# Rotary scores of multi-head latent attention: two mixed passes as one matmul, with high parts of the queries moved across partitions by transfers

## The chip, the core and the metric

The kernel runs on one core of one Trainium2 chip. Its engines are TensorE (PE, with its weight loads shown apart as PEld), VectorE (DVE), ScalarE (ACT), GpSimd (POOL) and SyncE (SP), each with a queue of its own that is worked off in order. The metric is the time of one execution on the device, in us.

## The reference, cut to what matters

One layer of an encoder over 256 tokens of width 2048, in float32: multi-head latent attention (MLA, 8 heads) and differential attention side by side, cross attention into 256 memory tokens, a gated feed-forward block and a last norm. The part that the change touches are MLA's scores. Each head has a part of 128 dimensions without rotation and a rotary part of 64, and all heads share one rotary key:

```python
q_rope = apply_rope(q[..., MLA_NOPE_DIM:], cos_r, sin_r)
k_rope = apply_rope(k_rope, cos_r, sin_r)
...
s = (jnp.einsum('bqhd,bkhd->bhqk', qn_b, k_nope)
     + jnp.einsum('bqhr,bkr->bhqk', qr_b, k_rope))
p = jax.nn.softmax(s.astype(jnp.float32) * scale, axis=-1).astype(v.dtype)
return jnp.einsum('bhqk,bkhd->bqhd', p, v)
```

## The kernel before

**Three passes.** Every float32 product is made on PE in the format float32r from two parts of each operand: h is the value rounded by ACT (L99, L102), l is what is left, subtracted by DVE (L100, L103). `mm` issues h x h, h x l and l x h into one PSUM sum (L91, L92, L93). `Split` is such a pair of tiles, `split_into` makes it, `act_tile` takes two buffers for it from the pool "act", which has 24 buffers of one size (128 partitions x 1024 float32).

**The steps of MLA.** The first projection gives the latents; `latents_normalized` norms them, rotates the shared key (`kr`) and transposes all to dimension-major form: cqT (queries' latent), and in one tile `lat` ckvT (keys' and values' latent) and krT (rotary key). `kr` is 256 wide with the key in columns 0 to 63 and again in 192 to 255 and zeros between, so krT has two planes: plane 0 has the key in partitions 0 to 63 and zeros in 64 to 127, plane 1 the other way round. The rotary queries of all heads come from one projection, are rotated (`qrs`) and transposed into qrT: plane j of qrT holds head 2j in partitions 0 to 63 and head 2j + 1 in 64 to 127. A head's rotary score takes the plane of its pair and the plane of krT for its parity; the zeros cut out the other head. So a head's scores are, for each of the two token tiles, three passes for the 128 dimensions (qT, kT) and three for the rotary part (qrT, krT).

The heads come in two groups of four (`hg`). For each group `stationary` makes qT and kT and `values` makes the values (tiles `val_h`, `val_l`, read out of the PSUM tiles `acc`). Then, pair of heads by pair, `scores` fills a PSUM tile psc, `softmax` takes the maximum (nm, DVE), the exponential (e, ACT, with its sum ssum), the reciprocal (rs) and scales (DVE); `prob_T` transposes the result on PE (ppt, L462 before, L495 after) and splits it into pT; `heads_out` multiplies with the values (po) into mixT.

**What stands around it.** acc_dq, the first projection of differential attention, is held in two of the four PSUM banks of the pool "pacc" until `diff_rope` reads it, after MLA's last value split (`issue_after(mla_split)`). The other two banks serve, one after the other, the rotary queries, the two groups' values and then the projection of dk (`diff_project(0, 1)`, matmuls acc<-..x0T), which is independent of MLA.

**What sets the order.** The kernel is written in Tile, and its scheduler puts the instructions of each engine in an order of its own by a time model, at build time; weight loads alone stay as written (`keep_in_program_order`). Buffers of a pool are given in the order in which tiles are asked for, and a tile whose buffer is still read by an earlier one waits for that reader. So the number of tiles asked for can change the order of all engines.

Of the kernel before, what the change touches and what calls it, by code (L numbers as in the profile page):

```python
# [11 lines left out]
F32 = mybir.dt.float32  # L12
F32R = mybir.dt.float32r
# [3 lines left out]
ALU = mybir.AluOpType  # L17
AX = mybir.AxisListType

P = 128  # L20
S = 256
# [9 lines left out]
DD = 128  # L31
DV = 256
XH = 4
# [41 lines left out]
def encoder_block(ctx: ExitStack, tc: tile.TileContext, a, out):  # L75
# [13 lines left out]
    def mm(o, l, r, start, stop):  # L89

        nc.tensor.matmul(o, l.h, r.h, start=start, stop=False)  # L91
        nc.tensor.matmul(o, l.h, r.l, start=False, stop=False)  # L92
        nc.tensor.matmul(o, l.l, r.h, start=False, stop=stop)  # L93
# [13 lines left out]
    def act_tile(shape=(P, 4, S), name="act"):  # L107
        return Split(
            act.tile(list(shape), F32R, name=name + "_h", tag="act"),
            act.tile(list(shape), F32R, name=name + "_l", tag="act"),  # L110
        )
# [57 lines left out]
    def ps_tile(name):  # L169
        return pps.tile([P, 512], F32, name=name, tag="ps")  # L170
# [140 lines left out]
    def transposed(dst, src, tt, n, gain=None, raw=None):  # L311

        pt = ps_tile("pt")
        for j in range(n):
            nc.tensor.transpose(out=pt[:, j * P:(j + 1) * P], in_=src[:, j * P:(j + 1) * P], identity=ident)  # L315
        pv = pt[:, :n * P].rearrange("p (j t) -> p j t", t=P)
        if gain is not None:
            g = nat("gT").rearrange("p (j t) -> p j t", t=P) if raw is None else raw[:, :, tt * P:(tt + 1) * P]
            nc.vector.tensor_tensor(out=g[:, :n, :], in0=pv, in1=gain.unsqueeze(2).to_broadcast([P, n, P]),
                                    op=ALU.mult)  # L320
            pv = g[:, :n, :]
        split_into(dst[:, :n, tt * P:(tt + 1) * P], pv)
# [27 lines left out]
    cosd = const.tile([P, NT, 2, DD // 2], F32, name="cosd")  # L350
    sind = const.tile([P, NT, 2, DD // 2], F32, name="sind")

    def latents_normalized():
        cqs = [nat("cq") for _ in range(NT)]
        for tt in range(NT):
            rms_rows(cqs[tt], acc_q[tt], tt, QL, QL, "rq")
        with tc.issue_after(last_cast[0]):
            for c_t, s_t, f0, f1 in ((cosr, sinr, 0, DR // 2), (cosd, sind, DR // 2, NF)):
                for h in range(2):
                    nc.scalar.activation(s_t[:, :, h, :], turns[:, :, f0:f1], AF.Sin, scale=two_pi if h else -two_pi)  # L360
                    nc.scalar.activation(c_t[:, :, h, :], prod[:, :, f0:f1], AF.Sin, scale=two_pi)
        for t in (cosd, sind):
            for tt in range(NT):
                nc.gpsimd.tensor_scalar(out=t[:, tt], in0=t[:, tt], scalar1=rstd1[:, tt:tt + 1], scalar2=None,
                                        op0=ALU.mult)
        ckvs = [nat("ckv") for _ in range(NT)]
        for tt in range(NT):
            rms_rows(ckvs[tt], acc_kv[tt], tt, KVL + DR, KVL, "rkv")
        for tt in range(NT):
            transposed(cqT, cqs[tt], tt, 4, g_q)  # L370
        for tt in range(NT):
            c = ckvs[tt]

            kr = nat("kr")
            nc.gpsimd.memset(kr[:, 64:192], 0.0)
            rope(kr[:, 0:64], c[:, 256:320], cosr[:, tt], sinr[:, tt], 1, 32)
            nc.gpsimd.tensor_copy(out=kr[:, 192:256], in_=kr[:, 0:64])
            transposed(ckvT, c, tt, 2, g_kv)
            transposed(krT, kr, tt, 2)


    acc_dq = project(x0T, [w_in[0, i] for i in range(4)], before=lambda i: i == 3 and latents_normalized())
# [32 lines left out]
            split_into(t[:, 2 * hp:2 * hp + 2, :], ps.rearrange("p (j t) -> p j t", j=2))  # L415
        return t

    qrT = act_tile(name="qrT")
    acc = project(lambda kt: cqT[:, kt, :], [a["w_uq_r"]])
    qrs = []  # L420
    for tt in range(NT):
        qr = nat("qr")
        rope(qr, acc[tt], cosr[:, tt], sinr[:, tt], NH, 32)
        qrs.append(qr)
    qT, kT, vv = [], [], []
    for hg in range(2):
        qT.append(stationary(weights(a["w_uq_n"][hg]), cqT, 4, "qT"))
        if hg == 0:
            for tt in range(NT):
                transposed(qrT, qrs[tt], tt, 4)  # L430
        kT.append(stationary(weights(a["w_ukv_k"][hg]), ckvT, 2, "kT"))
        vv.append(values(project(lambda kt: ckvT[:, kt, :], [a["w_ukv_v"][hg]])))
    mla_split = last_split[0]

    def scores(qs, ks):

        ps = ps_tile("psc")
        for tt in range(NT):
            for n, (q, k) in enumerate(zip(qs, ks)):
                mm(ps[:, tt * S:(tt + 1) * S], q[:, tt * P:(tt + 1) * P], k, n == 0, n == len(qs) - 1)  # L440
        return ps.rearrange("p (t k) -> p t k", t=NT)

    def softmax_parts(ps, scale):

        nm = small.tile([P, NT], F32, name="nm", tag="nm", bufs=4)
        nc.vector.tensor_reduce(out=nm, in_=ps, axis=AX.X, op=ALU.max, negate=True)
        nc.vector.tensor_scalar(out=nm, in0=nm, scalar1=scale, scalar2=None, op0=ALU.mult)
        e = soft.tile([P, NT, S], F32, name="e", tag="e", bufs=4)
        ssum = small.tile([P, NT], F32, name="ssum", tag="ssum", bufs=4)
        for tt in range(NT):  # L450
            nc.scalar.activation(e[:, tt, :], ps[:, tt, :], AF.Exp, bias=nm[:, tt:tt + 1], scale=scale,
                                 accum_out=ssum[:, tt:tt + 1])
        r = small.tile([P, NT], F32, name="rs", tag="rs", bufs=4)
        nc.vector.reciprocal(out=r, in_=ssum)
        return e, r
# [31 lines left out]
    for hg in range(2):  # L487
        t = act_tile(name="mixT")
        mixT.append(t)
        for hp in range(2):  # L490
            ps = [scores([qT[hg][:, h, :], qrT[:, 2 * hg + hp, :]], [kT[hg][:, h, :], krT[:, h % 2, :]])
                  for h in (2 * hp, 2 * hp + 1)]
            pTs = [prob_T(softmax(s, (DN + DR) ** -0.5)) for s in ps]
            heads_out(t[:, 2 * hp:2 * hp + 2, :], pTs, vv[hg], 2 * hp)
# [17 lines left out]
    def diff_attend(dq, dk, dv):  # L512
        mT = act_tile(name="diffT")
        ps_ = []
        for hh in range(2):
            (e1, r1), (e2, r2) = [
                softmax_parts(scores([dq[:, 2 * hh + c, :]], [dk[:, 2 * hh + c, :]]), DD ** -0.5) for c in range(2)]
            nr2 = small.tile([P, NT], F32, name="nr2", tag="nr2")
            nc.vector.tensor_scalar(out=nr2, in0=r2, scalar1=neg_lam, scalar2=None, op0=ALU.mult)
            for tt in range(NT):  # L520
                nc.vector.tensor_scalar(out=e1[:, tt, :], in0=e1[:, tt, :], scalar1=r1[:, tt:tt + 1], scalar2=None,
                                        op0=ALU.mult)
                nc.vector.scalar_tensor_tensor(out=e1[:, tt, :], in0=e2[:, tt, :], scalar=nr2[:, tt:tt + 1],
                                               in1=e1[:, tt, :], op0=ALU.mult, op1=ALU.add)
            ps_.append(e1)
        for hh in range(2):
            pT = prob_T(ps_[hh])
            po = ps_tile("pod")
            for tt in range(NT):
                for kt in range(NT):  # L530
                    mm(po[:, tt * DV:(tt + 1) * DV], pT[:, kt, tt * P:(tt + 1) * P],
                       dv[:, kt, hh * DV:(hh + 1) * DV], kt == 0, kt == NT - 1)
            ss = small.tile([P, NT], F32, name="ssd", tag="ssd")
            for tt in range(NT):
                meansq(po[:, tt * DV:(tt + 1) * DV], ss[:, tt:tt + 1], DV, DV)
            r = rstd_of(ss, 1e-5, "rd")
            on = nat("on")
            for tt in range(NT):
                nc.vector.scalar_tensor_tensor(out=on[:, tt * DV:(tt + 1) * DV], in0=po[:, tt * DV:(tt + 1) * DV],
                                               scalar=r[:, tt:tt + 1], in1=gdb, op0=ALU.mult, op1=ALU.mult)  # L540
            pt = ps_tile("pdt")
            for e in range(2):
                for tt in range(NT):
                    nc.tensor.transpose(out=pt[:, e * S + tt * P:e * S + (tt + 1) * P],
                                        in_=on[:, tt * DV + e * P:tt * DV + (e + 1) * P], identity=ident)
            split_into(mT[:, 2 * hh:2 * hh + 2, :], pt.rearrange("p (e t) -> p e t", e=2))
        return mT
# [71 lines left out]
        transposed(xqT, n, tt, 4)  # L619

    pxT = [act_tile(name="pxT") for _ in range(2)]
    ps = [scores([xqT[:, h, :]], [xkT[:, h, :]]) for h in range(XH)]
    for h in range(XH):
        prob_T(softmax(ps[h], XD ** -0.5), pxT[h // 2][:, h % 2 * 2:h % 2 * 2 + 2, :])
    xv = values(project(mT, [a["w_xv"][i] for i in range(4)]), rstdm)
# [380 lines left out]
```

## Time and profile before

| | |
|---|---|
| median of 3 runs | 1158.89 us (1158.38 to 1160.23) |
| the profiled execution: time of the run | 1158.9 us |
| the profiled execution: span | 1157.1 us |
| PE busy | 1148.1 us, 99%, 5510 matmuls |
| DVE busy | 901.3 us, 78% |
| ACT busy | 611.0 us, 53% |
| POOL busy | 69.3 us, 6% |
| granted TensorE clock over the span | 0.999 |

The span is counted from the first to the last instruction of the program; the run's time has 1.8 us around it. Busy times of PE overlap: matmuls are pipelined, and what one costs in a full queue is the distance between starts. In rows of the timeline the columns are start and duration in us, engine, line, operation, output tile and input tiles, shapes, count, and in brackets the idle time before it and what ended it. In the list of waits the columns are total us, times, and the longest.

### The profile page before, as it was taken

How to read it: one execution, taken by the hardware profiler on the slowest of the kernel's cores; microseconds unless marked ns; L12 is line 12 of the kernel's file. 1: busy time of each engine (PE TensorE's matmuls, PEld its weight loads, DVE VectorE, ACT ScalarE, POOL GpSimd, SP SyncE). 2: the span in 40 equal slices, each digit the busy share in tenths (PEclk: the TensorE clock that was granted, in tenths of full speed). 3: DMA queues.
4: the chain of work that ended last, by engine and by line, in shares of the span. 5: the costliest groups of instructions: out<-in, count | busy, mean ns of one | idle time of the engine just before them, and what ended most of it. 6: DMA issues, size and time to landing. Idle time of an engine off the chain costs nothing.

```text
span 1157.1 us, 14401 instructions
## 1 busy us (share of the span) xinstructions
PE 1148.1 (99%) x5510; PEld 961.7 (83%) x5510; DVE 901.3 (78%) x1197; ACT 611.0 (53%) x863; POOL 69.3 (6%) x81
## 2 busy tenths in 40 slices
PE   9999999999999999999999999999999999999997
PEld 7888888888888888888888888888888888888887
DVE  7698766586867776978888787797888788798873
ACT  6755454554665565655444554564544554554552
POOL 4920000001000000000000000000000000000021
PEclk9999999999999999999999999999999999999999
DMA  9565344435755445465565555645556555555651
GB/s 356 215 218 189 113 145 168 161 146 206 272 212 182 146 149 187 174 218 182 185 214 184 206 184 192 218 181 183 202 179 223 204 181 202 192 220 202 210 204 73
DMA packets 33764, 222.13 MB, mean 192 GB/s; under 512 B 4128, under 2 KB 4896, under 8 KB 8992
## 3 DMA queue, kind: packets, MB, share of 16 engines
q1 hardware_dynamic: 32256, 216.86, 52.4%
q0 software_dynamic: 864, 3.15, 0.7%
q10 hardware_dynamic: 576, 1.21, 0.3%
q8 instruction: 43, 0.70, 0.2%
q14 instruction: 25, 0.20, 0.1%
HBM read 219.11 MB, written 2.10 MB: 191 GB/s over the span
## 4 chain that ended last, share of the span: by engine, by line
PE 98%; DMA 1%; issue 0%; DVE 0%; SPq 0%; ACT 0%; POOLq 0%; POOL 0%; DVEq 0%; ACTq 0%
PE acc L92 28%; PE acc L91 28%; PE acc L93 28%; PE q L91 2%; PE q L92 2%; PE q L93 2%; PE pt L315 2%; PE ppt L462 1%; DMA wraw<-in_w_in_lat 1%; PE psc L93 1%; PE psc L91 1%; PE psc L92 1%; PE pt L838 0%; PE acckv L93 0%; PE acckv L92 0%
## 5 line engine op out<-in xcount | busy, mean ns | idle before, releaser
L99 ACT CAST wh<-wraw 128x1024 fp32r<-128x1024 f32 (+2 forms) x399 | 399.2, 1013 | 383.1 <-PE acc L93 346.7
L100 DVE TENSOR_TENSOR wl<-wraw,wh 128x1024 fp32r<-128x1024 f32 (+2 forms) x399 | 469.0, 1184 | 166.3 <-ACT wh L99 164.4
L92 PE MATMUL acc<-wl,x2n_h 128*128 128x512 f32 x480 | 185.5, 390 | 0.0
L93 PE MATMUL acc<-wh,x2n_l 128*128 128x512 f32 x480 | 185.2, 389 | 0.0
L91 PE MATMUL acc<-wh,x2n_h 128*128 128x512 f32 x480 | 160.3, 390 | 0.0
L93 PEld LDWEIGHTS acc<-wh,x2n_l 128*128 128x128 f32 x480 | 90.1, 188 | 18.8
L91 PEld LDWEIGHTS acc<-wh,x2n_h 128*128 128x128 f32 x480 | 90.1, 188 | 18.8
L92 PEld LDWEIGHTS acc<-wl,x2n_h 128*128 128x128 f32 x480 | 90.1, 188 | 18.7
L92 PE MATMUL acc<-wl,hT_h 128*128 128x512 f32 (+1 forms) x272 | 103.7, 381 | 0.0
L93 PE MATMUL acc<-wh,hT_l 128*128 128x512 f32 (+1 forms) x272 | 103.5, 381 | 0.0
L91 PE MATMUL acc<-wh,hT_h 128*128 128x512 f32 (+1 forms) x272 | 89.4, 382 | 0.0
L92 PE MATMUL acc<-wl,x0T_h 128*128 128x512 f32 x224 | 88.2, 395 | 0.0
L93 PE MATMUL acc<-wh,x0T_l 128*128 128x512 f32 x224 | 87.8, 393 | 0.0
L91 PE MATMUL acc<-wh,x0T_h 128*128 128x512 f32 x224 | 87.4, 396 | 0.3 <-ACT x0T_h L102 0.3
L99 ACT CAST wh<-tsum 128x1024 fp32r<-128x1024 f32 x56 | 58.3, 1047 | 42.2 <-DVE tsum L712 30.8
L100 DVE TENSOR_TENSOR wl<-tsum,wh 128x1024 fp32r<-128x1024 f32 x56 | 67.9, 1218 | 9.2 <-ACT wh L99 9.1
L91 PEld LDWEIGHTS acc<-wh,hT_h 128*128 128x128 f32 x272 | 51.2, 188 | 9.9 <-issue 0.2
L93 PEld LDWEIGHTS acc<-wh,hT_l 128*128 128x128 f32 x272 | 51.2, 188 | 9.6
L92 PEld LDWEIGHTS acc<-wl,hT_h 128*128 128x128 f32 x272 | 51.2, 188 | 9.4
L91 PEld LDWEIGHTS acc<-wh,x0T_h 128*128 128x128 f32 x224 | 42.2, 189 | 9.2 <-ACT x0T_h L102 1.2
L92 PEld LDWEIGHTS acc<-wl,x0T_h 128*128 128x128 f32 x224 | 42.3, 189 | 7.9 <-DVE wl L100 0.4
L93 PEld LDWEIGHTS acc<-wh,x0T_l 128*128 128x128 f32 x224 | 42.2, 188 | 7.6
(363 smaller groups left out, 2005.9 us busy)
## 6 DMA issues: line engine op xcount, KB each, us to landing
wraw<-in_w_gu SPq DMA_DIRECT2D x80, 1024.0 KB, 4.8
wraw<-in_w_dn SPq DMA_DIRECT2D x36, 1024.0 KB, 4.8
wraw<-in_w_in SPq DMA_DIRECT2D x24, 1024.0 KB, 4.8
wraw<-in_w_out SPq DMA_DIRECT2D x16, 1024.0 KB, 4.8
wraw<-in_w_down SPq DMA_DIRECT2D x8, 1024.0 KB, 4.8
wraw<-in_w_in_lat SPq DMA_DIRECT2D x7, 832.0 KB, 7.8
wraw<-in_w_xk SPq DMA_DIRECT2D x4, 1024.0 KB, 6.1
wraw<-in_w_xq SPq DMA_DIRECT2D x4, 1024.0 KB, 4.8
```

Of the source, the lines that this page charges most:

```text
L91: nc.tensor.matmul(o, l.h, r.h, start=start, stop=False)
L92: nc.tensor.matmul(o, l.h, r.l, start=False, stop=False)
L93: nc.tensor.matmul(o, l.l, r.h, start=False, stop=stop)
L99: last_cast[0] = nc.scalar.copy(out=dst.h, in_=src).ins
L100: last_split[0] = nc.vector.tensor_tensor(out=dst.l, in0=src, in1=dst.h.bitcast(F32), op=ALU.subtract).ins
L315: nc.tensor.transpose(out=pt[:, j * P:(j + 1) * P], in_=src[:, j * P:(j + 1) * P], identity=ident)
L462: nc.tensor.transpose(out=pt[:, kt * S + tt * P:kt * S + (tt + 1) * P], in_=p[:, tt, kt * P:(kt + 1) * P], identity=ident)
```

## The change

The product of the two mixed passes is summed over 64 dimensions, and the other 64 partitions of each pass hold zeros. The change puts both passes of a head into one matmul of 128 partitions. For heads of parity o, `qr_x[o]` holds in the head's own 64 partitions the low part of the query and in the other 64 its high part; `krT.l[:, o]` holds in the own partitions the high part of the key and in the others its low part. The sum over 128 partitions is then l x h + h x l. The pass h x h stays as it was. The high part of a query has to cross to the other 64 partitions, which engines' lanes don't do here: four transfers from SBUF to SBUF, issued by POOL, carry it (two parities, two token tiles). The keys need none, since `kr` holds the key in both halves.

So qrT's two tiles of the pool "act" become three (`qr_h`, `qr_x0`, `qr_x1`). `scores` takes the list of extra matmuls as an argument; its other two callers pass none and issue what they did.

```diff
@@ new function, in place of transposed(krT, kr, tt, 2)
+    def rope_keys(kr, tt):
+
+        pt = ps_tile("pt")
+        for j in range(2):
+            nc.tensor.transpose(out=pt[:, j * P:(j + 1) * P], in_=kr[:, j * P:(j + 1) * P], identity=ident)
+        pv = pt[:, :2 * P].rearrange("p (j t) -> p j t", t=P)
+        tok = slice(tt * P, (tt + 1) * P)
+        nc.scalar.copy(out=krT.h[:, :, tok], in_=pv)
+        for o in range(2):
+            own = slice(o * 64, o * 64 + 64)
+            nc.scalar.copy(out=krT.l[own, o, tok], in_=pv[own, o])
+            nc.vector.tensor_tensor(out=krT.l[own, 1 - o, tok], in0=pv[own, o],
+                                    in1=krT.h[own, o, tok].bitcast(F32), op=ALU.subtract)
...
-            transposed(krT, kr, tt, 2)
+            rope_keys(kr, tt)
...
-    qrT = act_tile(name="qrT")
+    qr_h = act.tile([P, 4, S], F32R, name="qr_h", tag="act")
+    qr_x = [act.tile([P, 4, S], F32R, name=f"qr_x{o}", tag="act") for o in range(2)]
...
+    def rope_queries(src, tt):
+        pt = ps_tile("pt")
+        for j in range(4):
+            nc.tensor.transpose(out=pt[:, j * P:(j + 1) * P], in_=src[:, j * P:(j + 1) * P], identity=ident)
+        pv = pt.rearrange("p (j t) -> p j t", t=P)
+        tok = slice(tt * P, (tt + 1) * P)
+        nc.scalar.copy(out=qr_h[:, :, tok], in_=pv)
+        for o in range(2):
+            own, other = slice(o * 64, o * 64 + 64), slice((1 - o) * 64, (1 - o) * 64 + 64)
+            nc.vector.tensor_tensor(out=qr_x[o][own, :, tok], in0=pv[own], in1=qr_h[own, :, tok].bitcast(F32),
+                                    op=ALU.subtract)
+            nc.gpsimd.dma_start(out=qr_x[o][other, :, tok], in_=qr_h[own, :, tok])
...
-                transposed(qrT, qrs[tt], tt, 4)
+                rope_queries(qrs[tt], tt)
...
-    def scores(qs, ks):
+    def scores(q, k, rope=()):
...
         for tt in range(NT):
-            for n, (q, k) in enumerate(zip(qs, ks)):
-                mm(ps[:, tt * S:(tt + 1) * S], q[:, tt * P:(tt + 1) * P], k, n == 0, n == len(qs) - 1)
+            tok = slice(tt * P, (tt + 1) * P)
+            o = ps[:, tt * S:(tt + 1) * S]
+            mm(o, q[:, tok], k, True, not rope)
+            for n, (l, r) in enumerate(rope):
+                nc.tensor.matmul(o, l[:, tok], r, start=False, stop=n == len(rope) - 1)
...
-            ps = [scores([qT[hg][:, h, :], qrT[:, 2 * hg + hp, :]], [kT[hg][:, h, :], krT[:, h % 2, :]])
+            ps = [scores(qT[hg][:, h, :], kT[hg][:, h, :],
+                         [(qr_h[:, 2 * hg + hp, :], krT.h[:, h % 2, :]),
+                          (qr_x[h % 2][:, 2 * hg + hp, :], krT.l[:, h % 2, :])])
```

The scheduler's order moves with it. Up to MLA's first scores PE's order differs by two matmuls of the values. After that it differs until the first projections of differential attention are done, and is the same from there on. The places that matter:

PE before, from the last scores of heads 0 and 1 on (psc_1105 is head 1's PSUM tile, acc_1460 and acc_1461 the two PSUM tiles of the projection of dk, wh and wl its weights):

```order
L91 MATMUL psc_1105<-lat_h_487,qrT_h_764 128x256
L92 MATMUL psc_1105<-lat_l_488,qrT_h_764 128x256
L93 MATMUL psc_1105<-lat_h_487,qrT_l_765 128x256
L91 MATMUL acc_1460<-wh_1464,x0T_h_112 128x512 [waits DVE_49]
L92 MATMUL acc_1460<-wl_1465,x0T_h_112 128x512
L93 MATMUL acc_1460<-wh_1464,x0T_l_113 128x512
...
L91 MATMUL acc_1460<-wh_1468,x0T_h_112 128x512 [waits Activation_49]
```

PE in the change at the same place (psc_1116 is head 1's tile, e_1130 and e_1150 the exponentials of heads 0 and 1, acc_1457 the dk projection's tile):

```order
L473 MATMUL psc_1116<-lat_h_487,qr_h_770 128x256
L473 MATMUL psc_1116<-lat_l_488,qr_x1_772 128x256 [waits DMASW3_49]
L495 MATMUL ppt_1138<-ident_98,e_1130 128x128 [waits DVE_49,PE_49]
L495 MATMUL ppt_1138<-ident_98,e_1130 128x128 [waits DVE_49]
L495 MATMUL ppt_1138<-ident_98,e_1130 128x128 x2
L495 MATMUL ppt_1158<-ident_98,e_1150 128x128 [waits DVE_49,PE_49]
L495 MATMUL ppt_1158<-ident_98,e_1150 128x128 [waits DVE_49]
L495 MATMUL ppt_1158<-ident_98,e_1150 128x128 x2
L91 MATMUL po_1167<-pT_h_1143,val_h_967 128x256 [waits Activation_49]
...
L473 MATMUL psc_1193<-lat_l_488,qr_x1_772 128x256
L91 MATMUL acc_1457<-wh_1461,x0T_h_112 128x512 [waits DVE_49]
```

Before, the dk projection follows the scores, and 57 of its matmuls stand ahead of the transposes of e. In the change the transposes of e follow at once, then scores of heads 2 and 3 and the products with the values, and the dk projection comes behind all scores of the first group.

DVE before, around the split of the second group's values (val_l_1085, out of acc_1064 and acc_1065), which is followed by the rotation of dq (ropetmp, dn) and then by the maximum of head 0 (nm_1118):

```order
L100 TENSOR_TENSOR kT_l_1033<-kT_1049,kT_h_1032 128x512 [waits Activation_49]
L100 TENSOR_TENSOR val_l_1085<-acc_1064,val_h_1084 128x512 [waits Activation_49]
L100 TENSOR_TENSOR val_l_1085<-acc_1065,val_h_1084 128x512 [waits Activation_49]
L305 TENSOR_TENSOR ropetmp_1433<-acc_514,sind_513 128x4x64
L307 TENSOR_TENSOR dn_1432<-acc_514,cosd_512 128x4x64
...
L446 TENSOR_REDUCE nm_1118<-psc_1092 128x2 [waits PE_49]
```

DVE in the change (val_l_1098 is the same split; nm_1127 and nm_1204 are the maxima of heads 0 and 2, kT_l_1046 the second group's key, wl_1500 a part of the dk projection's weights):

```order
L100 TENSOR_TENSOR kT_l_1046<-kT_1062,kT_h_1045 128x512 [waits Activation_49]
L479 TENSOR_REDUCE nm_1127<-psc_1105 128x2 [waits PE_49]
L100 TENSOR_TENSOR wl_1500<-wraw_1493,wh_1499 128x1024 [waits Activation_49]
...
L487 RECIPROCAL rs_1134<-ssum_1131 128x2 [waits Activation_49]
L506 TENSOR_SCALAR e_1130<-e_1130,rs_1134 128x256 [waits DVE_49]
...
L100 TENSOR_TENSOR pT_l_1144<-ppt_1138,pT_h_1143 128x512 [waits Activation_49]
...
L479 TENSOR_REDUCE nm_1204<-psc_1182 128x2 [waits PE_49]
L480 TENSOR_SCALAR nm_1204<-nm_1204 128x2 [waits DVE_49]
L100 TENSOR_TENSOR val_l_1098<-acc_1077,val_h_1097 128x512 [waits PE_49]
L100 TENSOR_TENSOR val_l_1098<-acc_1078,val_h_1097 128x512
L305 TENSOR_TENSOR ropetmp_1430<-acc_514,sind_513 128x4x64
```

The split of the values and the rotation of dq moved behind the softmax of heads 0 and 1 and the maximum of head 2, and the split, which waited for ACT, now waits for PE.

POOL in the change, between the work on gdb and the first reciprocal root of differential attention; the four transfers are new and nothing else moved on this queue:

```order
L544 TENSOR_SCALAR gdb_1424<-gdb_1424 128x256 [waits DMAHW1_49]
L453 DMA qr_x0_771<-qr_h_770 64x4x128 [waits Activation_49]
L453 DMA qr_x1_772<-qr_h_770 64x4x128
L453 DMA qr_x0_771<-qr_h_770 64x4x128 [waits Activation_49]
L453 DMA qr_x1_772<-qr_h_770 64x4x128
```

The queue of SP is the same in both.

More of the change, by code (lines that the diff above doesn't have):

```diff
@@ L516, in diff_attend @@
             (e1, r1), (e2, r2) = [
-                softmax_parts(scores([dq[:, 2 * hh + c, :]], [dk[:, 2 * hh + c, :]]), DD ** -0.5) for c in range(2)]
+                softmax_parts(scores(dq[:, 2 * hh + c, :], dk[:, 2 * hh + c, :]), DD ** -0.5) for c in range(2)]
             nr2 = small.tile([P, NT], F32, name="nr2", tag="nr2")
@@ L621, in encoder_block @@
     pxT = [act_tile(name="pxT") for _ in range(2)]
-    ps = [scores([xqT[:, h, :]], [xkT[:, h, :]]) for h in range(XH)]
+    ps = [scores(xqT[:, h, :], xkT[:, h, :]) for h in range(XH)]
     for h in range(XH):
```

## The prediction

> **What bounds the kernel now.** I read the page's header and engine shares first, then the chain that ended last, then the list of waits of TensorE, and last the timeline around the rotary scores.
>
> ```profile
> span 1157.1 us, 14401 instructions
> PE 1148.1 (99%) x5510; PEld 961.7 (83%) x5510; DVE 901.3 (78%) x1197; ACT 611.0 (53%) x863; POOL 69.3 (6%) x81
> PE 98%; DMA 1%; issue 0%; DVE 0%; SPq 0%; ACT 0%; POOLq 0%; POOL 0%; DVEq 0%; ACTq 0%
> ```
>
> ```profile
> PE wps L197 <- DVE warm L191: 1.2, 1, 1.2
> PE acc L91 <- ACT x0T_h L102: 0.3, 1, 0.3
> PE po L91 <- ACT val_h L102: 0.2, 1, 0.2
> ```
>
> 98% of the chain is PE. The second block is TensorE's whole list of waits: it waited three times, none of them in MLA. So the time is the sum of the issue slots of PE's instructions. A removed matmul is worth one slot, and every us in which PE's queue stands still is lost.
>
> The sum is made against this execution: span 1157.1, run 1158.9. The median shown, 1158.89, is the same number. 0.2% is 2.3 us, about what a measurement can tell from no change.
>
> **The saving.** One head's scores before, and the first matmul after the scores of heads 0 and 1:
>
> ```profile
> 95.58 0.28 PE L91 MATMUL psc<-kT_h,qT_h 128*128 128x256 f32 x1
> ...
> 96.17 0.28 PE L93 MATMUL psc<-lat_h,qrT_l 128*128 128x256 f32 x1
> 96.29 0.28 PE L91 MATMUL psc<-kT_h,qT_h 128*128 128x256 f32 x1
> ...
> 98.45 0.40 PE L91 MATMUL acc<-wh,x0T_h 128*128 128x512 f32 x1
> 111.75 0.93 PE L462 MATMUL ppt<-ident,e 128*128 128x128 f32 x7
> ```
>
> ```profile
> L93 PE MATMUL psc<-lat_h,qrT_l x16: 278/283/283, 96.2 to 151.5; 128*128 128x256 f32 x16
> ```
>
> Columns of the timeline: start, duration. A score matmul is recorded with 0.28, but the next starts 0.12 later, and that is its price. 16 go (8 heads, 2 token tiles): 16 x 0.12 = 1.9 us less. Matmuls with zeros or with mixed halves have the same shape, so the same slot.
>
> **The new buffer.** The pool "act" has 24 buffers of one size. When the second head group's values are made, 24 are held before the change: x0T 8, lat 2, qrT 2, and qT, kT, val of two groups 4 each. Now qr_h, qr_x0 and qr_x1 take three where qrT took two: 25. The last one asked for, val_l of the second group, must wait until one is given back, and the first to be given back is kT_l of the first group, after head 3's scores. The order shows exactly this wait on PE. Behind val_l stand, on DVE, the rope of dq, and on PE the projection of dk, whose PSUM banks val_l has to read out first. That projection is what filled PE (98.45 above, then 57 matmuls) while the softmax of heads 0 and 1 ran. In the new order these heads' transposes follow their scores at once. So PE waits through a bare softmax. Its length comes from these rows, the first block DVE around the place, the second the softmax of cross attention, where ACT goes from one head to the next:
>
> ```profile
> 95.14 0.68 DVE L100 TENSOR_TENSOR kT_l<-kT,kT_h 128x512 fp32r<-128x512 f32 x1
> 95.74 1.34 DVE L100 TENSOR_TENSOR val_l<-acc,val_h 128x512 fp32r<-128x512 f32 x2
> ...
> 99.65 0.68 DVE L446 TENSOR_REDUCE nm<-psc 128x2 f32<-128x512 f32 x1
> 100.25 1.21 DVE L100 TENSOR_TENSOR wl<-wraw,wh 128x1024 fp32r<-128x1024 f32 x1
> ...
> 107.26 0.62 DVE L473 TENSOR_SCALAR e<-e,rs 128x256 f32<-128x256 f32 x2
> ```
>
> ```profile
> 392.43 0.16 DVE L447 TENSOR_SCALAR nm<-nm 128x2 f32<-128x2 f32 x1
> 392.68 0.47 ACT L451 ACTIVATE e<-psc,nm 128x256 f32<-128x256 f32 x1 [2.63 <-DVE nm L447]
> ...
> 394.05 0.48 ACT L451 ACTIVATE e<-psc,nm 128x256 f32<-128x256 f32 x1
> 394.40 0.21 ACT L451 ACTIVATION_READ_ACCUMULATOR e<-psc,nm 128x1 f32 x1
> 394.65 0.17 DVE L454 RECIPROCAL rs<-ssum 128x2 f32<-128x2 f32 x1
> 394.85 0.61 DVE L473 TENSOR_SCALAR e<-e,rs 128x256 f32<-128x256 f32 x2
> ```
>
> Worked in the new order, with the first score at 95.58 as before (the work ahead is the same, two matmuls apart in place): head 0's ten scores end at 95.58 + 9 x 0.12 + 0.28 = 96.94, head 1's at 98.14; PE has issued all at 97.98. DVE: maximum of head 0 at 96.98; one weight split that stands behind it in its queue, 97.58 (1.13 to the next); the scale of the maximum 98.71; maximum of head 1 98.78. ACT: two exponentials of head 0 from 98.95, 0.45 apart, sum read by 99.95; head 1 by 100.86. DVE: reciprocal 100.0, both halves scaled by 100.8. PE transposes head 0: one after the first half, three from 100.85. Idle: 100.85 - 97.98 - 0.11 (that transpose's slot; 7 took 0.93) = 2.8 us. Head 1: scaled by 101.7, three of four transposes from 101.76; PE was free at 101.18 and did one in between: 0.5 us. Then scores of heads 2 and 3 (10 + 10 slots) cover the split of the probabilities. kT_l's last reader starts near 104.9, ends 105.1; val_l's first half is done at 105.9, and PE comes to the dk projection at 105.9: 0 to 0.2. Sum of idle time 3.4 us.
>
> How fast PE starts again after a wait is seen once before:
>
> ```profile
> 406.66 0.69 ACT val_h L102
> ```
>
> ```profile
> 407.40 0.39 PE L91 MATMUL po<-pxT_h,val_h 128*128 128x256 f32 x1 [0.16 <-ACT val_h L102]
> 407.63 0.28 PE L92 MATMUL po<-pxT_l,val_h 128*128 128x256 f32 x1
> ```
>
> 0.05 after the work it waited for, and a first slot of 0.23 for 0.12. Three restarts with and without this: 3.2 to 3.9. If DVE's weight split were not in the way, 1.1 less: 2.3 is the low end. I take 3.4. After that 43 projection matmuls stand ahead of the next transposes: 106 + 43 x 0.23 = 116. With DVE's other work between, the first two heads' softmax took 99.65 to 107.9 before, 8.2 us; head 2's maximum now starts near 103.7, so it is ready near 112. I expect no second idle stretch.
>
> **The other edits.** The four transfers and the extra small work:
>
> ```profile
> 81.60 1.07 ACT L99 CAST qrT_h<-pt 128x512 fp32r<-128x512 f32 x2
> 81.65 0.86 POOL L509 TENSOR_SCALAR gdb<-gdb 128x256 f32<-128x256 f32 x1
> 83.18 1.28 DVE L100 TENSOR_TENSOR qrT_l<-pt,qrT_h 128x512 fp32r<-128x512 f32 x2
> 90.43 2.36 DVE L100 TENSOR_TENSOR wl<-wraw,wh 128x1024 fp32r<-128x1024 f32 x2 [1.40 <-ACT wh L99]
> ```
>
> ```profile
> L577 POOL DMA_DIRECT2D mn<-in_mem x4: 537/542/790, 285.7 to 287.5; - x4
> DMA to landing us min/median/max: 6.4/7.6/11.0
> ```
>
> POOL has nothing queued behind gdb that anyone awaits soon; it issues four transfers of 128 KB from 82.5, 0.54 to 0.79 each, the last by 85.7 at most. No transfer between buffers exists before; the nearest are POOL's four of 512 KB: 6.4 to 11.0. So the last lands between 90.5 and 96.7, its reader stands at 97.9: hidden, with 1.2 us to spare at the worst row. I take 0. The qr_x subtractions run on 64 partitions but the same 512 columns: four of 0.60 instead of two, 1.2 us more DVE, ahead of a 1.40 us wait of DVE that swallows it; without it the later weight splits would move 1.2. The keys' casts and subtractions (six small ones more, 0.27 to 0.4 by the 128x256 rows' kind, about 2 us on two engines around 69 to 77 us) lie beside matmuls that never waited. 0.
>
> Sum: -1.9 + 3.4 = +1.5 us: 1158.9 + 1.5 = **1160.4**.
>
> **Rivals.**
> 1. PE's clock falls in the stall: slower beyond the bound. What the trace has on idle stretches:
>
> ```profile
> 1.18 3.59 PE L197 MATMUL wps<-warm 128*128 128x512 bf16 x8 [1.18 <-DVE warm L191]
> 7.32 0.63 PE L93 MATMUL acc<-wh,x0T_l 128*128 128x512 f32 x2
> 1149.90:1153.90 4.00, 0.00 (x0) 0.00 (x0) 2.16 (x6) 0.94 (x1) 0.55 (x1) 1.00 0.61 232
> 1154.00:1157.00 3.00, 0.00 (x0) 0.00 (x0) 0.00 (x0) 0.00 (x0) 0.00 (x0) 0.50 0.49 193
> ```
>
> At the start matmuls were 0.42 apart ((3.59 - 0.6)/7), until about 7.3; at the end the granted clock stayed 1.00 for 4.0 us without a matmul, then went to 0.50. A stall of 2.8 is shorter than 4.0, which speaks against. If it did happen, at most 6 us at half rate: 3.0 us, 1163.4. It decides if a granted clock below 1 shows after 98 us.
> The Trainium skill, "TensorE: Matmul & The Clock Gate", Part 1, states that the clock is halved after at least one idle window of about 3.4 us and comes back after a busy one. An estimate by it: 1.7 us lost, 1162.1 in all; the trace's 4.0 us at full clock agrees with a window that must be idle throughout.
> 2. Transfers late: landing at 14 us or more, so past 97.9, moves scores and all behind by the excess; at twice the quoted maximum of 11.0 (22, from 85.7) about 10 us, at 14 to 16 about 2: 1162 to 1163. Against it: a quarter of the bytes.
> 3. The stall is covered, the change only saves: 1157.0. It would need PE to have other work between the scores and the transposes; its queue is in order, and none stands there.
> 4. The idle stretches add up to over 4.2 (further waits in the second head group, whose order changed too): 1161.5 to 1162.5.
>
> **Chances.** The forecast 0.70; rival 1 0.07, rival 2 0.07, rival 3 0.06, rival 4 0.10. Slower by over 0.2% (above 1161.2) are rivals 1 and 2, most of 4, and the upper end of the forecast (idle 4.2 of 2.3 to 4.4): 0.14 + 0.08 + 0.06 = 0.28. Faster by over 0.2% would need more than the 1.9 saved: 0.03. The rest 0.69. Low end of the range: idle 2.3, and 0.9 for the spread of runs: 1158.4; high end: 1163.0, near the ends of rivals 1 and 2.
>
> **What would show it.** Right: the waits list has PE ppt waiting for DVE e, 2.5 to 3.5 in all, and DVE val_l or a wait on PE psc that was not there; PE starts the dk projection near 106 instead of 98.5; psc matmuls are 80 instead of 96 in MLA; PE still full elsewhere. Wrong: a wait of PE for a transfer at qr_x, a granted clock below 1 after 98, a wait in the second head group, or no PE wait at the transposes.

## The result and the profile after

| | before | after |
|---|---|---|
| median | 1159.41 us (8 runs, 1158.38 to 1160.23) | 1162.62 us (8 runs, 1161.13 to 1163.36) |
| profiled execution: time, span | 1158.9, 1157.1 us | 1162.65, 1160.9 us |
| granted TensorE clock over the span | 0.999 | 0.997 |

The ratio is 1.0026, 95% interval 1.0015 to 1.0036: about 3 us slower. The forecast was 1160.4 with 1158.4 to 1163.0. The range held, but the centre was 2.2 us too low, and "slower by over 0.2%" had a chance of 0.28 only. Of the 2.2 us, 0.5 is the kernel before, whose median over these 8 runs lies above the 1158.9 that the forecast started from; 1.7 is the change, 3.2 us between the medians instead of 1.5.

The page of the changed kernel, header, engines and chain:

```profile
span 1160.9 us, 14393 instructions
PE 1148.5 (99%) x5494; PEld 962.0 (83%) x5494; DVE 903.5 (78%) x1201; ACT 612.1 (53%) x867; POOL 70.8 (6%) x85
PE 98%; DVE 1%; issue 0%; ACT 0%; DMA 0%; POOLq 0%; POOL 0%; DVEq 0%; ACTq 0%
```

16 matmuls fewer, yet PE is busy 0.4 us longer, and DVE has come onto the chain with 1%. TensorE's list of waits says where:

```profile
PE ppt L495 <- DVE e L506: 2.6, 1, 2.6
...
PE qT L91 <- DVE qr_x L451: 0.6, 1, 0.6
```

Beside the three that stood there before, two waits are new: the one at the transposes (forecast), and one at qT (not forecast). PE's timeline around the first:

```profile
99.35 0.28 PE L473 MATMUL psc<-lat_l,qr_x 128*128 128x256 f32 x1
102.22 2.00 PE L495 MATMUL ppt<-ident,e 128*128 128x128 f32 x8 [2.59 <-DVE e L506]
103.97 0.58 PE L91 MATMUL po<-pT_h,val_h 128*128 128x256 f32 x1
104.35 0.42 PE L91 MATMUL psc<-kT_h,qT_h 128*128 128x256 f32 x1
104.57 0.41 PE L92 MATMUL psc<-kT_l,qT_h 128*128 128x256 f32 x1
...
105.32 0.28 PE L91 MATMUL psc<-kT_h,qT_h 128*128 128x256 f32 x1
...
108.28 0.28 PE L473 MATMUL psc<-lat_l,qr_x 128*128 128x256 f32 x1
108.40 0.50 PE L91 MATMUL acc<-wh,x0T_h 128*128 128x512 f32 x1
```

After the last score of head 1 (99.35 + 0.12) PE stands still for 2.75 us. Then a transpose takes 0.22 ((103.97 - 102.22)/8) instead of 0.11, and a score 0.22 (104.35 to 104.57) instead of 0.12, until 105.2. The dk projection starts at 108.40, behind the scores of heads 2 and 3. The same stretch in windows; after the length stand the busy times of PE, PEld, DVE, ACT and POOL (in brackets their instructions), then the granted clock, the DMA share and GB/s:

```profile
98.34:101.74 3.40, 1.29 (x11) 1.08 (x10) 2.85 (x7) 1.75 (x7) 0.00 (x0) 1.00 0.09 14
101.75:105.16 3.41, 2.94 (x13) 2.57 (x14) 2.35 (x7) 1.82 (x6) 0.00 (x0) 0.50 0.77 298
105.20:108.60 3.40, 3.40 (x29) 3.36 (x29) 2.17 (x5) 1.26 (x5) 0.00 (x0) 1.00 0.00 0
```

The clock was halved for one stretch of 3.41 us right behind one in which PE was busy for 1.29 us of 3.40. What it costs, in distances between starts: eight transposes 1.75 instead of 0.87, the first po matmul 0.38 instead of 0.12, four scores 0.85 instead of 0.48: 1.5 us. Of the 0.38 up to 0.16 is not the clock: the po matmul's weight load waited that long for ACT's pT_h.

The second wait, PE before the change and after it, then DVE after it:

```profile
84.07 0.28 PE L93 MATMUL kT<-lat_h,wl 128*128 128x256 f32 x1
84.19 0.28 PE L91 MATMUL qT<-cqT_h,wh 128*128 128x256 f32 x1
```

```profile
84.80 0.28 PE L93 MATMUL kT<-lat_h,wl 128*128 128x256 f32 x1
85.63 0.35 PE L91 MATMUL qT<-cqT_h,wh 128*128 128x256 f32 x1 [0.56 <-DVE qr_x L451]
```

```profile
84.10 2.81 DVE L451 TENSOR_TENSOR qr_x<-pt,qr_h 64x512 fp32r<-64x512 f32 x4
```

The second group's first qT tile takes over a PSUM bank of the transposed rotary queries (pt). That bank is now read by two subtractions on DVE, 0.7 each, where one of 0.64 stood before. The two that read the first bank take from 84.10 to about 85.5, and PE starts at 85.63: 0.83 after the last kT matmul instead of 0.12, 0.71 us lost.

The sum: -1.9 (16 slots) + 0.71 + 2.75 + 1.5 + 0.1 (the first slot of the dk projection, 0.33 for 0.23) = +3.2, against +3.2 between the medians. In the two profiled executions 0.7 us more had passed already before these places (the kT rows, 84.07 and 84.80). Over the ten traces that row lies between 83.7 and 85.2, and for kernels with the change on both sides of the kernel before, so this is put down to the start of a run and not to the change.

### The profile page after: what moved, and what is told of

The parts are those of the page before. It is cut to its first block, busy times and chain, and to the rows that moved or that the text cites. A ratio compares the mean times of both kernels' runs of the same rounds, so it can differ in the third digit from the quotient of the medians.

```text
span 1160.9 us, 14393 instructions
## 1 busy us (share of the span) xinstructions
PE 1148.5 (99%) x5494; PEld 962.0 (83%) x5494; DVE 903.5 (78%) x1201; ACT 612.1 (53%) x867; POOL 70.8 (6%) x85
## 4 chain that ended last, share of the span: by engine, by line
PE 98%; DVE 1%; issue 0%; ACT 0%; DMA 0%; POOLq 0%; POOL 0%; DVEq 0%; ACTq 0%
PE acc L91 28%; PE acc L93 28%; PE acc L92 28%; PE q L91 2%; PE q L92 2%; PE q L93 2%; PE pt L315 2%; PE ppt L495 1%; PE acckv L91 0%; PE acckv L92 0%; PE acckv L93 0%; PE psc L93 0%; PE psc L92 0%; PE psc L91 0%; PE pt L873 0%
```

## The experiments

The theory that the trace gives is A: the changed kernel needs one buffer more than the pool has. That alone puts the dk projection behind the softmax, and the wait makes the clock fall. C is the theory of the wait at qT: PE waits there for a PSUM bank that two subtractions read in place of one. Against A stands B: the mixed passes, the transfers or the small work cost the time.

### 25 buffers

```diff
-    act = ctx.enter_context(tc.tile_pool(name="act", bufs=24))
+    act = ctx.enter_context(tc.tile_pool(name="act", bufs=25))
-        return sb.tile([P, 512], F32, name=name, tag="nat", bufs=7)
+        return sb.tile([P, 512], F32, name=name, tag="nat", bufs=6)
-    invf = const.tile([P, NF], F32, name="invf")
+    invf = tp.tile([P, NF], F32, name="invf")
```

> The changed kernel with 25 buffers in the pool act instead of 24; to make room, the pool of the 512-wide tiles (nat) has 6 instead of 7 buffers and one small table lives in the tables' pool. Theory A (the twenty-fifth buffer alone puts the projection of dk behind the softmax, and the wait that follows lets PE's clock fall): PE's list of waits has no ppt waiting for DVE e, the first matmul acc<-wh,x0T_h starts right behind head 1's scores, the granted clock stays 1.00 between 95 and 110 us, and only the wait of 0.6 to 0.7 at qT for qr_x is left. Time: 1159.4 - 1.9 + 0.7 = 1158.2, 4.4 less than the changed kernel. Rival B (the mixed passes, the transfers or the extra small work cost the time): the time stays at 1161.5 or more, with waits at psc or slots of the new matmul (lat_l,qr_x) over 0.12.

Measured: 1157.32 us (11 runs, 1157.04 to 1158.36) against 1159.01 of before, ratio 0.9989 (0.998 to 0.9997). The one wait that its list has beside the three of before, then PE where the dk projection starts, and a window behind it:

```profile
PE qT L91 <- DVE qr_x L451: 0.2, 1, 0.2
```

```profile
99.40 0.28 PE L473 MATMUL psc<-lat_l,qr_x 128*128 128x256 f32 x1
99.52 0.40 PE L91 MATMUL acc<-wh,x0T_h 128*128 128x512 f32 x1
```

```profile
101.00:104.00 3.00, 3.00 (x15) 2.49 (x14) 3.00 (x7) 0.00 (x0) 0.00 (x0) 1.00 0.00 0
```

The wait at the transposes is gone, the projection follows the scores at once, the clock is 1.00. The mixed passes and the transfers are all still there. B falls: its 1161.5 is 4 us off. The two edits that make room (one buffer of "nat" fewer, a table in another pool) are part of this run; that the number of buffers in "act" decides, as A says, is shown together with the run with 23 buffers below, where nothing else differs. The ratio to the changed kernel is 0.9989/1.0026 = 0.996, 4.3 us less where 4.4 was expected; the two intervals lie apart.

### 25 buffers and one subtraction per token tile

```diff
-        for o in range(2):
-            own, other = slice(o * 64, o * 64 + 64), slice((1 - o) * 64, (1 - o) * 64 + 64)
-            nc.vector.tensor_tensor(out=qr_x[o][own, :, tok], in0=pv[own], in1=qr_h[own, :, tok].bitcast(F32),
-                                    op=ALU.subtract)
-            nc.gpsimd.dma_start(out=qr_x[o][other, :, tok], in_=qr_h[own, :, tok])
+        lo, hi = slice(0, 64), slice(64, P)
+        nc.vector.tensor_tensor(out=qr_x[0][:, :, tok], in0=pv, in1=qr_h[:, :, tok].bitcast(F32), op=ALU.subtract)
+        nc.gpsimd.tensor_copy(out=qr_x[1][hi, :, tok], in_=qr_x[0][hi, :, tok].bitcast(F32))
+        nc.gpsimd.dma_start(out=qr_x[1][lo, :, tok], in_=qr_h[hi, :, tok])
+        nc.gpsimd.dma_start(out=qr_x[0][hi, :, tok], in_=qr_h[lo, :, tok])
```

> As the kernel with 25 buffers, but per token tile one subtraction over 128 partitions on DVE instead of two over 64; POOL copies the odd heads' low parts from qr_x0 to qr_x1, and then two transfers bring the high parts as before. Theory C (the qT matmuls wait for the PSUM bank that DVE's two subtractions per tile hold for twice as long): the wait of PE at qT for qr_x goes, 0.6 to 0.7 less than with 25 buffers alone: 1157.5. Rival D (the wait there comes from the cast qr_h on ACT or from the transposes themselves): the wait stays, 1158.2. A second rival (POOL's copies make the transfers land later than the scores need them): a wait at psc of 1 to 3 us, 1159 to 1161.

Measured: 1157.11 us (11 runs, 1156.45 to 1158.01), ratio to before 0.9984 (0.9975 to 0.9993). The list of waits has only the three of before, and PE goes from kT to qT without a gap:

```profile
83.66 0.28 PE L93 MATMUL kT<-lat_h,wl 128*128 128x256 f32 x1
83.78 0.28 PE L91 MATMUL qT<-cqT_h,wh 128*128 128x256 f32 x1
```

C is shown in the trace: without the second reader of the bank the wait is gone. In time the step can't be told from the kernel with 25 buffers (0.2 us between the medians). That kernel's own gap at this place was 0.39 in its trace and not 0.71; over the six traces with two subtractions the gap is 0.39 to 1.10 us. In each of them PE starts 1.53 or 1.54 us after DVE's first subtraction, so the gap depends on how far PE has come by then. By its median this is the lowest version, and it is below both kernels.

### The shortage alone, in the kernel before

```diff
-    act = ctx.enter_context(tc.tile_pool(name="act", bufs=24))
+    act = ctx.enter_context(tc.tile_pool(name="act", bufs=23))
```

> The kernel before with 23 buffers in the pool act, one too few for it as 24 are for the changed kernel; nothing of the scores is changed. Theory A: the same picture as in the changed kernel, ppt waits 2.5 to 2.8 for DVE e, val_l of the second group waits for kT_l's last reader, the granted clock falls to 0.5 for one stretch of about 3.4 us: 2.75 + 1.5 = 4.3 more than before, 1163.7; if the clock doesn't fall, 2.75 + 0.5 = 3.3 more, 1162.7. Rival B (the shortage alone does little, the change's own work is needed for it): within 1 us of before, 1158.9 to 1160.4.

Measured: 1163.41 us (5 runs, 1162.71 to 1164.27), ratio 1.0038 (1.0025 to 1.0051), 4.4 us more. PE, and the windows at the place:

```profile
97.94 0.28 PE L93 MATMUL psc<-lat_h,qrT_l 128*128 128x256 f32 x1
100.57 0.72 PE L462 MATMUL ppt<-ident,e 128*128 128x128 f32 x4 [2.35 <-DVE e L473]
101.48 0.72 PE L462 MATMUL ppt<-ident,e 128*128 128x128 f32 x4 [0.19 <-DVE e L473]
...
108.33 0.50 PE L91 MATMUL acc<-wh,x0T_h 128*128 128x512 f32 x1 [0.31 <-DVE val_l L100]
```

```profile
98.71:102.12 3.41, 1.36 (x9) 1.05 (x10) 2.51 (x10) 2.52 (x9) 0.00 (x0) 1.00 0.72 231
102.13:105.53 3.40, 3.40 (x18) 3.40 (x18) 1.69 (x3) 0.58 (x1) 0.00 (x0) 0.50 0.17 70
```

The same picture without anything of the change: the wait (2.51 us beyond the slot), the late dk projection, the halved clock. So the shortage suffices. Here head 1's transposes ran at full clock, and head 1's own wait shows (100.57 to 101.48 for four transposes, some 0.4 too much). In the changed kernel the half clock covered it. The clock fell at 102.12, when PE had been at work again for 1.5 us.

### The saving alone, in the kernel before

```diff
-                mm(ps[:, tt * S:(tt + 1) * S], q[:, tt * P:(tt + 1) * P], k, n == 0, n == len(qs) - 1)
+                o, l = ps[:, tt * S:(tt + 1) * S], q[:, tt * P:(tt + 1) * P]
+                nc.tensor.matmul(o, l.h, k.h, start=n == 0, stop=False)
+                if n == 0:
+                    nc.tensor.matmul(o, l.h, k.l, start=False, stop=False)
+                nc.tensor.matmul(o, l.l, k.h, start=False, stop=n == len(qs) - 1)
```

> The kernel before without one of the two mixed passes of the rotary part (the query's high part by the key's low part is left out): 16 matmuls of 128x256 less, no new buffer, no transfer, no other order of the work around the scores. Theory: 16 x 0.12 = 1.9 us less, 1157.5, and the first matmul of the dk projection starts 0.5 us earlier against the first score (4 of the 16 stand in heads 0 and 1). Rival: a score pass that follows on the same stationary or the same PSUM sum costs less than a slot, or the time saved is waited for at the transposes: 0 to 1 less, 1158.4 to 1159.4.

Measured: 1157.46 us (11 runs, 1156.81 to 1158.11), ratio 0.9987 (0.9978 to 0.9996): 1.5 us less, interval 0.5 to 2.5; 1.9 expected. PE, first score, last score of head 1, and the dk projection:

```profile
95.57 0.28 PE L441 MATMUL psc<-kT_h,qT_h 128*128 128x256 f32 x1
...
97.84 0.28 PE L444 MATMUL psc<-lat_h,qrT_l 128*128 128x256 f32 x1
97.96 0.40 PE L91 MATMUL acc<-wh,x0T_h 128*128 128x512 f32 x1
```

From the first score to the projection 2.39 us, where the kernel before took 98.45 - 95.58 = 2.87: four slots of 0.12. The saving is what was forecast, and the kernels with 25 buffers keep it.

### The wait filled with work

```diff
-    def prob_T(p, t=None):
+    def prob_T(p, t=None, fill=0):
         pt = ps_tile("ppt")
+        for _ in range(fill): nc.tensor.matmul(pt[:, :S], kT[0].h[:, 0, :P], kT[0].h[:, 0, :], start=True, stop=True)
...
-            pTs = [prob_T(softmax(s, (DN + DR) ** -0.5)) for s in ps]
+            pTs = [prob_T(softmax(s, (DN + DR) ** -0.5), fill=20 * ((hg, hp, j) == (0, 0, 0))) for j, s in enumerate(ps)]
```

> The changed kernel (24 buffers) with 20 extra matmuls of 128x256 ahead of the first transposes of head 0; they read kT_h, wait for nothing, and write a part of the PSUM tile that the transposes overwrite. They take 20 x 0.12 = 2.4 of the 2.75 us in which PE waits there, so the wait for e stays but PE works through it. Theory A (PE idle for most of one 3.4 us stretch lets the clock fall, which costs 1.5 us): the granted clock stays 1.00 after 98 us, the transposes follow each other at 0.11 instead of 0.21, head 1's wait of 0.5 comes back, and PE reaches the end of head 1's transposes about 1 us earlier against the first score. In all 1161.6, if the order of the later work, which also moves somewhat, costs nothing. Rival B (the 0.21 slots come from the restart after a wait or from contention, not from the clock): the transposes stay at 0.21 and the time at 1162.6.

Measured: 1160.95 us (10 runs, 1160.67 to 1162.01), ratio to before 1.0016 (1.0007 to 1.0026), 1.2 us less than the changed kernel by the ratios, whose intervals overlap. PE at the place, and two windows:

```profile
98.40 0.28 PE L473 MATMUL psc<-lat_l,qr_x 128*128 128x256 f32 x1
98.52 2.56 PE L492 MATMUL ppt<-kT_h 128*128 128x256 f32 x20
101.19 0.81 PE L495 MATMUL ppt<-ident,e 128*128 128x128 f32 x4
102.19 0.72 PE L495 MATMUL ppt<-ident,e 128*128 128x128 f32 x4 [0.19 <-DVE e L506]
102.67 0.39 PE L91 MATMUL po<-pT_h,val_h 128*128 128x256 f32 x1
...
103.48 0.28 PE L91 MATMUL psc<-kT_h,qT_h 128*128 128x256 f32 x1
```

```profile
98.00:101.00 3.00, 3.00 (x26) 2.88 (x24) 2.58 (x7) 1.48 (x7) 0.00 (x0) 1.00 0.23 55
101.00:104.00 3.00, 2.70 (x20) 2.23 (x20) 2.30 (x7) 1.63 (x4) 0.00 (x0) 1.00 0.72 295
```

PE works through the wait, the clock stays 1.00, and head 1's own wait comes back. From the last score of head 1 to the sixth score of head 2 it is 103.48 - 98.40 = 5.08 us; in the changed kernel 105.32 - 99.35 = 5.97. So 20 matmuls of no use make the kernel 0.9 us shorter at this place: the clock, less head 1's wait that it covered. This run alone can't tell the clock from the rival (slow slots from the restart), since it has no long wait to restart from. The kernel with 23 buffers can: there PE restarted at 100.57, four transposes took 0.49 us (101.48 to 101.97), and the scores' slots were 0.22 from 102.23 on, behind the fall of the clock at 102.12. Contention, the rival's other half, does not fit either: the DMA share in the half-clock stretch was 0.77 in the changed kernel and 0.17 with 23 buffers, and the slots were the same. The order of the work behind 104 us moves too in this kernel, so the local figure is the firmer one.

The same edit with 8 and with 14 extra matmuls:

> As the kernel with 20 extra matmuls ahead of head 0's transposes, with 8: 0.96 us of the wait is filled, 1.8 us stays idle. If the clock falls only after a stretch of 3.4 us of which more than half is idle (2.1 us and 1.9 us so far with a fall), it stays 1.00 here, or falls where the stretch happens to begin with the wait; if any idle time over 0.7 us is enough, it falls.

> As the kernel with 20 extra matmuls ahead of head 0's transposes, with 14: 1.7 us of the wait is filled, 1.1 us stays idle. By a share of half or more of a 3.4 us stretch the clock stays 1.00; it falls if about 1 us is enough.

Each ran once, 1162.07 us with 8 and 1160.70 with 14, so the times say little. With 8:

```profile
98.82:102.23 3.41, 1.87 (x16) 1.61 (x14) 2.99 (x8) 1.85 (x8) 0.00 (x0) 1.00 0.24 60
102.24:105.64 3.40, 3.20 (x25) 2.87 (x25) 2.68 (x7) 1.25 (x3) 0.00 (x0) 1.00 0.60 248
```

Neither has a halved clock between 98 us and the end of the program. With 8, PE was idle for 1.54 us (3.41 - 1.87) of a stretch of 3.41 us that the changes of the clock mark out (the first comes at 6.66 in this trace, and 6.66 + 27 x 3.4133 = 98.82), and the clock stayed. In the changed kernel 2.11 us were idle, in the kernel with 23 buffers 2.05 (not the 1.9 of the expectation), and it fell. With 14, the stretch at this place had 1.0 us idle.

### Transfers that land late

```diff
             nc.gpsimd.dma_start(out=qr_x[o][other, :, tok], in_=qr_h[own, :, tok])
+            nc.gpsimd.dma_start(out=qr_x[o][other, :, tok], in_=qr_h[own, :, tok])
```

This was done in the kernel with 25 buffers.

> The kernel with 25 buffers and each of the four transfers issued twice; the second copy goes to the same place and waits for the first one's landing, so the last data land one transfer later. Theory (a transfer lands 6.3 us after its issue, the first round between 90 and 92.8, and its first reader stands at 97.5): the second round lands between 96 and 99.5, PE now waits 0.5 to 2 us at psc for qr_x, and the time is 1158 to 1159.5; with one round the margin of 4.7 us hides them. Rival (the transfers cost by contention with the weights' loads or with DVE and ACT, not by their landing): no wait of PE at psc, but weight loads or splits later, and the time the same or up by less than 0.5.

Measured: 1159.22 us (10 runs, 1156.81 to 1162.87), ratio to before 1.0005 (0.9993 to 1.0018), 1.9 us more than with one round, by ratios whose intervals just overlap. POOL's issues and the wait in the list of PE's waits:

```profile
82.30 2.70 POOL L453 DMA_DIRECT2D qr_x<-qr_h  x4
88.44 0.61 POOL L454 DMA_DIRECT2D qr_x<-qr_h  x1 [3.44 <-DMA qr_x<-qr_h]
90.25 1.81 POOL L454 DMA_DIRECT2D qr_x<-qr_h  x3 [1.20 <-DMA qr_x<-qr_h]
```

```profile
PE psc L474 <- DMA qr_x<-qr_h: 0.3, 1, 0.3
```

The first transfer of the first round had landed by 88.44, and the last of the second was issued by 92.06. PE's first reader of qr_x, at 96.36 in this trace, did not wait; the second started at 97.82 instead of 97.32, and the last, whose weight load waited for the same transfers, at 99.05 instead of 98.76: 0.8 us in all. The order of the scores moved too (head 1's first three stand ahead of that second reader). So late landing is shown, at the place and in the size that the theory gave. That contention costs nothing beside it is not shown. The spread of 6 us is far wider than the 1.3 of the kernel with one round, and the profiled execution, 1158.1, is one of the short ones. Of the four runs above 1161 three have a mean granted clock of 0.996 or 0.997, the others all 0.998 or 0.999; a longer wait there that also cost the clock would give that, but there is no trace of these runs.

## Why the prediction was right or wrong

The main mechanism was right: one buffer too few, head 0's wait, the late dk projection. That the range held is partly luck. The forecast's own terms end at 1158.9 - 1.9 + 4.4 = 1161.4, below the measured 1162.6; the range went on to 1163.0 for rivals 1 and 2. Rival 1, with a chance of 0.07, is what came, beside a term that the sum had at nothing; and the sign of being wrong that the prediction named, a granted clock below 1 after 98, showed.

**The saving, -1.9: right.** The slot of 0.12 held for the mixed matmul as for the others, and leaving the 16 out alone gave -1.5 (0.5 to 2.5).

**The new buffer, head 0's wait of 2.8: right, in cause and size.** 2.75 was measured. The DVE rows of the changed kernel read as the working did, with a weight split (wl) between the maximum and its scale:

```profile
98.47 0.69 DVE L479 TENSOR_REDUCE nm<-psc 128x2 f32<-128x512 f32 x1 [0.69 <-PE psc L473]
99.08 1.21 DVE L100 TENSOR_TENSOR wl<-wraw,wh 128x1024 fp32r<-128x1024 f32 x1
100.21 0.16 DVE L480 TENSOR_SCALAR nm<-nm 128x2 f32<-128x2 f32 x1
...
101.72 0.62 DVE L506 TENSOR_SCALAR e<-e,rs 128x256 f32<-128x256 f32 x2
...
107.65 1.29 DVE L100 TENSOR_TENSOR val_l<-acc,val_h 128x512 fp32r<-128x512 f32 x2 [0.65 <-PE psc L92]
```

The last row is the wait that the order promised, val_l for PE's last reader of kT_l. The runs with 25 and with 23 buffers show that the number of buffers decides. The 0 to 0.2 at the dk projection was 0.1. No further idle stretch came in the second head group (rival 4).

**Head 1's wait of 0.5: not seen, but not wrong.** The half clock made the transposes so slow that the data were there in time. With PE kept busy it was back (102.19, behind DVE e).

**Rival 1, the clock: the step that failed.** It had a chance of 0.07, since the granted clock stayed 1.00 through 4.0 us without a matmul at the end of the trace and the wait was only 2.8. That reading took the length of an idle stretch for what counts, and one end of one trace for its bound. At the ends of the ten traces the clock falls between 2.3 and 4.4 us after the last matmul's end, so 4.0 us at full clock was one draw out of this range. What the runs show is the idle share of a stretch of 3.41 us that begins where it happens to begin: 2.05 and 2.11 us idle were enough, 1.54 were not. It cost 1.5 us, half of the 3.0 put up as a bound. The Trainium skill, "TensorE: Matmul & The Clock Gate", Part 1, whose rule gave an estimate of 1.7 in the prediction, comes near in the price. Its condition, at least one idle window of about 3.4 us, does not cover this case: PE was busy for 1.29 us of the window, and the measurement decides.

**"The qr_x subtractions: 0": wrong by 0.7.** The step looked for who waits for DVE's later work and found a pause of 1.40 us that would swallow 1.2. Each subtraction took 0.70, where 0.60 was put down. The step did not ask who waits for the operands of the work itself: the PSUM bank is free only when its last reader is done, and the next tile for that bank belongs to PE. With one reader the wait is gone.

**The transfers, 0: right.** They landed well ahead:

```profile
83.37 2.71 POOL L453 DMA_DIRECT2D qr_x<-qr_h  x4
...
DMA to landing us min/median/max: 6.3/6.6/7.3
```

Issued by 85.5 and landed by 92.8 at the latest, against a first reader at 97.55; the forecast bounds were 90.5 to 96.7 and 97.9. No wait of PE names them. Rival 2 did not come; with the transfers doubled PE waited for them.

**The keys' small work, 0:** no wait of PE names it in any of the kernels that have it.

**Rival 3, 1157.0 if the wait were covered,** is about what the change is worth with a buffer more: 1157.1 to 1157.3.

In sum: -1.9 and the waits of head 0 and the dk projection stood; the half clock took 1.5 where the sum had 0.5 for head 1's wait, and the subtractions took 0.7 where it had 0. That is the whole difference between +1.5 and +3.2.

## What to carry to other kernels

Count the buffers that a change holds at the busiest moment against the pool: here one buffer too few put 57 matmuls of cover behind the softmax, and turned a gain of 1.3 us (1.9 with the single subtraction) into a loss of 3. When a work item on an idle engine grows, ask first who takes over what it reads, the PSUM bank above all, and only then who is queued behind it. An idle stretch of PE of more than about 2 us may cost the clock on top of its own length, so a wait that can't be removed is better filled.

## What the runs showed of the hardware

The granted clock fell to 0.50 for exactly one stretch of 3.41 us after a stretch of that length in which PE was idle for 2.05 us (23 buffers) or 2.11 us (the change), and did not fall after 1.54 us (8 extra matmuls). So a stretch need not be idle throughout; the bound lies between 45% and 60% idle by these three. The changes of the clock lie on a grid of 3.41 us (in the changed kernel 9.59, 101.75 and 105.16, and 101.75 - 9.59 = 27 x 3.4133), whose place against the program differs from run to run (9.59 here, 6.55 with 23 buffers).

The ends of the programs, where PE has nothing left to do, agree. With 23 buffers:

```profile
1153.43:1156.83 3.40, 1.14 (x10) 0.94 (x8) 2.12 (x8) 1.11 (x3) 0.55 (x1) 1.00 0.75 288
1156.85:1159.85 3.00, 0.00 (x0) 0.00 (x0) 0.65 (x2) 0.31 (x1) 0.00 (x0) 0.50 0.78 303
```

In all ten traces the last fall comes on the grid of that trace, behind a stretch that was idle for 66% or more (2.26 of 3.40 us here), and the stretches ahead of it, idle for 30% at most, had no fall. So the twelve falls all stand behind 60% or more, and the highest share without one is the 45%.

The same wait may therefore cost the clock in one run and not in another. The mean granted clock is 0.998 or 0.999 in the eight traces without a fall in the middle, and 0.997 and 0.996 in the two with one. Of the changed kernel's 8 runs seven had 0.997 and one, the fastest at 1161.13, 0.998. Of the 5 runs with 23 buffers the fastest, 1162.71, had 0.999, and 1162.7 was expected there without a fall. That these two runs kept their clock is likely, but they were not traced. Whether the bound depends on where in the stretch the idle time lies stays open.
